# Norm 1's factors amid V, dt's softplus a unit sooner, decay sums inside z, x's convolution behind z's splits

## The chip, the cores and the metric

One Trainium2 chip, one NeuronCore of it. The metric is device time in microseconds of one launch, the median of several runs. Engines are named as in the profile: PE is TensorE (matrix products; PEld its weight loads), DVE is VectorE, ACT is ScalarE, POOL is GpSimd, and SP is SyncE, which here only issues DMAs.

## What is computed

One hybrid decoder layer on 256 tokens of width 1024, in float32. What matters here is its beginning: norm 1, one combined input projection, and the SSD mixer with its `dt`.

```python
hn = rmsnorm(x, norm1_w)
proj = hn @ w_in
z, xbc_raw, dt_raw, q, k, v, g_raw = jnp.split(proj, IN_OFFSETS, axis=-1)
xbc = jax.nn.silu(causal_dwconv(xbc_raw, conv_w, conv_b))
xs, Bm, Cm = jnp.split(xbc, [SSD_D_INNER, SSD_D_INNER + SSD_GN], axis=-1)
dt = jax.nn.softplus(dt_raw + dt_bias)
Adt = dt * -jnp.exp(a_log)
A_cs = jnp.cumsum(Adt, axis=-1)      # per chunk of 128 tokens
L = jnp.exp(segsum(Adt))
y_diag = jnp.einsum('bclgn,bcsgn->bcgls', Cc, Bc) * L  @ (X * dt)
...
```

There are 32 SSD heads in 8 groups and 16 attention heads. After the mixer and the attention come the merge gates, an output projection, a ConvFFN with its own norm, and a last norm; the change touches none of these.

## The kernel before

**Units of weights.** Every projection is cut into units of 1 MB of weights: 8 pieces along the depth of 1024, each of 128 rows by 256 columns. SP loads a unit into one of three buffers `raw` (`load_raw`, line 90). Products are float32 by parts: ScalarE rounds half a unit (4 pieces) to its high part `hi` (`split_high`, line 95), VectorE subtracts to get the low part `lo` (`split_half`, line 101), and TensorE then does three products for each piece and column half: high by high, high by low, low by high (`mm_unit`, lines 160 to 162). A unit is thus 48 products. There are four buffers each for `hi` and `lo`. `next_unit` loads ahead and splits one unit ahead, so that a unit's splits are traced while the unit before it is multiplied.

**The order of the units.** For each of 8 groups `g`: B and C (`u_bc`), x (`u_x`), q and k (`u_qk`), z (`u_z`), and in turn V or the merge gates (`u_gate`). V's first unit and the first half of unit 0 (B and C of group 0) are special: they are multiplied before the splits are there, in plain float32.

**The head.** The input comes in four loads. `prepare` (lines 299 to 302) squares two pieces of x on ScalarE, scales them by the norm's weights on VectorE into `xw`, and adds the two squares. TensorE does V's products with the unnormalised `xw` (`v_raw`, line 289, two products a piece), the sums of squares with a column of ones (`stats`, line 306), and between them idle products (`idle`, line 295), whose result nobody reads. Then come the root (line 321, ScalarE), and the factor `rstd1` (lines 322 to 326, VectorE), dt's raw products (line 329), the factor's broadcast to all partitions (`rms_bcast`, line 237), and two idle products. `normed` (line 336) multiplies by the factor on VectorE, and the plain products of unit 0 (line 347) follow it piece by piece; then ScalarE and VectorE split the normalised input (`high`, `low`, lines 339 and 342) and the weights, and TensorE ends unit 0 with split products. In this stretch TensorE, ScalarE and VectorE keep the program's order.

**After the head.** From line 638 on only TensorE keeps the program's order. The order of ScalarE's and VectorE's queues is chosen when the kernel is built, by a planner that goes by what is ready and by priority (program order, unless a block is marked `high_priority`); `issue_after(i)` puts a block's instructions on the engine of `i` behind `i` in that engine's queue. `hn_end` holds the last high and the last low split of the head. `conv_silu` (lines 379 to 389) starts on ScalarE (`cacc`), does three taps for each of two halves on VectorE, a tanh on ScalarE, and a product on VectorE. `dt_chain` (line 597) turns dt's raw rows with four narrow instructions of TensorE (line 600) and then makes the softplus and dt times A in some twenty small steps, a chain on VectorE with two steps of ScalarE. `dt_sums` (line 622) makes the running sums over a chunk on TensorE, `dt_turn` (line 630) transposes them, copies them and writes them to DRAM on POOL's queue, and `load_acs` reads them back as a broadcast to all partitions (`acsB`). From these `s_mx` (line 469) makes the decay factors: twelve pieces on ScalarE, one exponential, and a product with B·C on VectorE. The scan's products `s_y` of group `g` are done behind x's unit of group `g + 1`.

**Banks.** Three PSUM banks pass round among the units' outputs (`mm_tile`); a unit's output holds one until the last of its readers is through. Other banks carry the tags `ss` (2), `at` (2) and `acc` (1).

**What the change touches:** `split_half`, the loop around `v_raw`, the place of `rms_bcast` and of dt's turn, `conv_silu`, `u_x`, `u_qk`, `u_z`, `s_mx`, `dt_chain`, and in the group loop what is done for `g` 0 and 1.

Of the kernel before, what the change touches and what calls it, by code (L numbers as in the profile page):

```python
# [8 lines left out]
F32 = mybir.dt.float32  # L9
F32R = mybir.dt.float32r  # L10
I32 = mybir.dt.int32
AF = mybir.ActivationFunctionType
# [29 lines left out]
def block_kernel(tc, xtok_d, head_d, par_d, nf_d, con_d, rope_d, win_d, wgate_d, bg_d, watt_d, wssd_d, wout_d, wup_d, wdn_d, out_d):  # L42
# [3 lines left out]
    with st:  # L46
# [33 lines left out]
        def col(c):  # L80
            return par[:, c : c + 1]
# [11 lines left out]
        def split_high(raw, k0, n):  # L93
            hi = wpool.tile([P, 4, 256], F32R, tag="hi", bufs=4, name="hi")
            split_half.hi = nc.scalar.activation(hi[:, :n], raw[:, k0 : k0 + n], AF.Copy)  # L95
            return hi

        def split_half(raw, k0, n, hi=None):
            hi = hi or split_high(raw, k0, n)
            lo = wpool.tile([P, 4, 256], F32R, tag="lo", bufs=4, name="lo")  # L100
            split_half.lo = nc.vector.tensor_tensor(lo[:, :n], raw[:, k0 : k0 + n], hi[:, :n].bitcast(F32),  # L101
                                                    op=ALU.subtract)
            return hi, lo, n

        def split_unit(raw, nk=KD):

# [174 lines left out]
        with tc.manual_schedule(engines=IN_ORDER):  # L281
# [22 lines left out]
            def stats(k, first=False, last=False):  # L304
                for c in range(2):
                    nc.tensor.matmul(stat[:, 0, c : c + 1], sq[:, k, c * P : c * P + P], ones[:, 0:1],
                                     start=(first and c == 0), stop=(last and c == 1))

            for k in range(0, KD, 2):
                prepare(k)  # L310
            for k in range(0, KD, 2):
                v_raw(k)
                if k == 6:
                    stats(6, last=True)
                v_raw(k + 1)
                if k < 6:
                    stats(k, first=(k == 0))
                    idle((3, 2, 1)[k // 2])

            mh, root, rr = n1[:, 0], n1[:, 1], n1[:, 2]  # L320
            nc.scalar.activation(root, stat[:, 0, 0:2], AF.Sqrt, scale=1.0 / D, bias=eps)
# [2 lines left out]
            nc.vector.tensor_tensor(rr, root, root, op=ALU.mult)  # L324
            nc.vector.tensor_tensor(rr, rr, mh, op=ALU.mult)
            nc.vector.scalar_tensor_tensor(rstd1, rr, 1.5, root, op0=ALU.add, op1=ALU.mult)
            for k in range(KD):
                j = NH * (k % 4)
                nc.tensor.matmul(ps_dt[j : j + NH, 0, :], wdt[:, k], xw[:, k], start=(k < 4), stop=(k >= KD - 4))
            rb1 = rms_bcast(rstd1)  # L330
            idle(2)

            psbc = mm_tile()

# [18 lines left out]
            for k in range(4, KD):  # L353
                low(k)
            half0 = split_half(raws[0], 4, 4, hi)
            mm_unit(psbc, [half0], hn, first=False, k0=4)
            nc.scalar.activation(dtp, ps_dt[:, 0, :], AF.Copy)
            for c in range(2):
                nc.scalar.activation(vt0[:, c], psv[:, c], AF.Identity, scale=rstd1[:, c : c + 1])
            for k in range(4):  # L360
# [9 lines left out]
                nc.vector.tensor_scalar(par[:, a:b], par[:, a:b], 0.5, None, op0=ALU.mult)  # L370


        def conv_silu(dst, src, cts, urgent=False):
# [3 lines left out]
            with tc.high_priority() if urgent else ExitStack():  # L377
                for m in range(2):
                    i = nc.scalar.activation(accs[m], src[:, m], AF.Identity, bias=col(C_CB + cts[m]), scale=w(m, 3))  # L379
            conv_silu.first = i  # L380
            for m in range(2):
                acc = accs[m]
                for s in (1, 2, 3):
                    i = nc.vector.scalar_tensor_tensor(acc[:, s:], src[:, m, : T - s], w(m, 3 - s), acc[:, s:],  # L384
                                                       op0=ALU.mult, op1=ALU.add)
                conv_silu.taps = i
# [9 lines left out]
        def u_bc(g):  # L396
            hv = next_unit()
            ps = mm_tile() if g else psbc
            if g:
                mm_unit(ps, hv, hn)  # L400
            bc = S[g]["bc"] = ssp.tile([P, 2, T], F32, tag="bc", bufs=1, name="bc")
            conv_silu(bc, ps, (16 + g, 24 + g), urgent=(g == 1))

        def u_x(g):
            hv = next_unit()
            ps = mm_tile()
            mm_unit(ps, hv, hn)
            xs = S[g]["xs"] = ssp.tile([P, 2, T], F32, tag="xs", bufs=2, name="xs")
            conv_silu(xs, ps, (2 * g, 2 * g + 1))

        def load_acs(g):
            acsB = S[g]["acsB"] = ssp.tile([P, 4, T], F32, tag="acsB", bufs=1, name="acsB")
# [1 line left out]

        def u_qk(g):
            hv = next_unit()
            ps = mm_tile()
            mm_unit(ps, hv, hn)
            raw = atp.tile([P, 2, T], F32, tag="qkraw", bufs=1, name="qkraw")
            S[g]["qk_copy"] = nc.scalar.activation(raw, ps, AF.Copy)  # L420
            sw = swaps[g % 2]
            nc.gpsimd.dma_start(sw[48:80:2], raw[49:80:2])
            nc.gpsimd.dma_start(sw[49:80:2], raw[48:80:2])
            qk = S[g]["qk"] = atp.tile([P, 2, T], F32, tag="qk", bufs=2, name="qk")
            cosb = rope[:, 0:1, :].to_broadcast([P, 2, T])
            nc.vector.tensor_tensor(qk, raw, cosb, op=ALU.mult)
# [22 lines left out]
            vt = S[g - 1]["vt"] = S[g]["vt"] = ssp.tile([P, 2, T], F32, tag="vt", bufs=2, name="vt")  # L449
            nc.scalar.activation(vt, ps, AF.Copy)  # L450

        def u_z(g):
            hv = next_unit()
            ps = mm_tile()
            mm_unit(ps, hv, hn)
            zt = S[g]["zt"] = ssp.tile([P, 2, T], F32, tag="zt", bufs=2, name="zt")
            S[g]["z_tanh"] = nc.scalar.activation(zt, ps, AF.Tanh, scale=0.5)
            nc.vector.scalar_tensor_tensor(flat(zt), flat(zt), 1.0, flat(ps), op0=ALU.add, op1=ALU.mult)
# [7 lines left out]
            nc.vector.tensor_tensor(cb, pcb[:, 0:3], mmask, op=ALU.mult)  # L466
            S[g]["cb"] = cb

        def s_mx(g, behind, conv=()):
# [5 lines left out]
            def factors(r):  # L475
                h = 4 * g + r
                for c, b in ((0, 0), (1, 2)):
                    nc.scalar.activation(mx[:, r, b], acsB[:, r, c * P : c * P + P], AF.Relu, scale=-1.0,
                                         bias=acs[:, c, h : h + 1])
                nc.scalar.activation(mx[:, r, 1], acsB[:, r, P:T], AF.Exp, bias=alm[:, h : h + 1])  # L480

            with ExitStack() as order:
                order.enter_context(tc.issue_after(behind.ins))
                factors(0)
                factors(1)
                if conv:
                    order.enter_context(tc.high_priority())
                    order.enter_context(tc.issue_after(conv[0].ins))
                    order.enter_context(tc.issue_after(conv[1].ins))
                factors(2)  # L490
                factors(3)
                nc.scalar.activation(mx[:, :, 0:3:2], mx[:, :, 0:3:2], AF.Exp, scale=-1.0)
                m2 = mx.rearrange("p h b l -> p h (b l)")
                nc.vector.tensor_tensor(m2, m2, flat(cb)[:, None, :].to_broadcast([P, 4, 3 * P]), op=ALU.mult)

        def s_xt(g):
            xs = S[g]["xs"]
# [97 lines left out]
        b3 = lambda ap: ap[:, None, :].to_broadcast([P, 2, NH])  # L595
        r3 = lambda i: dtw[:, i].rearrange("p (c h) -> p c h", c=2)
        def dt_chain():
            ps = ps_s.tile([P, 2, T], F32, tag="ss", bufs=2, name="ps_dt2")
            for c in range(2):
                nc.tensor.matmul(ps[:, 0, c * NH : c * NH + NH], dtp[:, c * P : c * P + P], sel, start=True, stop=True)  # L600
            for c in range(2):
                nc.vector.scalar_tensor_tensor(dtw[:, 0, c * NH : c * NH + NH], ps[:, 0, c * NH : c * NH + NH],
                                               rstd1[:, c : c + 1], par[:, C_DTB : C_DTB + NH], op0=ALU.mult, op1=ALU.add)
            nc.scalar.activation(dtw[:, 1], dtw[:, 0], AF.Abs)
            nc.scalar.activation(dtw[:, 2], dtw[:, 1], AF.Exp, scale=-1.0)
# [87 lines left out]
        for g in range(NG):  # L693
            if g:
                u_bc(g)
                with ExitStack() as order:
# [364 lines left out]
```

## Time and profile before

| | us |
|---|---|
| median of 3 runs (600.14 to 601.01) | 600.63 |
| the profiled execution, its time | 600.57 |
| the profiled execution, its span in the trace | 598.8 |
| TensorE busy in the span | 586.7 |
| VectorE busy | 459.7 |
| ScalarE busy | 375.9 |

The trace covers the span; the 1.8 us that the time has over it lie around the span. Times in rows are microseconds from the span's start. In timelines an entry in brackets is the idle time of the engine in front of the instruction, and what ended it. A row can merge several alike instructions (x8); its length is then that of the whole run of them. Matmuls overlap: one is shown with 0.28 us, yet the next starts 0.12 later.

### The profile page before, as it was taken

Reading aid. Unit: us, or ns where it says so; the run is one execution under the profiler, and the core shown is the slowest. Engines: PE = TensorE matmul, PEld = TensorE weight load, DVE = VectorE, ACT = ScalarE, POOL = GpSimd, SP = SyncE. Lnnn points to the kernel's source line nnn. Section 1 sums busy time; section 2 is a strip of 40 time slices with the busy share of each in tenths; the row PEclk is TensorE's granted clock in tenths of the full one; section 3 lists DMA queues with packets and bytes.
Section 4 is the critical chain, followed back from the end, with each engine's and each line's share of the span. In section 5 each row is a group of like instructions: output and inputs, shape, how many; then the busy total and the mean of one; then the engine's idle time right before and its main releaser. Section 6 shows DMA issues by size and latency. Waiting matters only on the chain.

```text
span 598.8 us, 9952 instructions
## 1 busy us (share of the span) xinstructions
PE 586.7 (98%) x3840; PEld 526.2 (88%) x3840; DVE 459.7 (77%) x891; ACT 375.9 (63%) x673; POOL 21.2 (4%) x41
## 2 busy tenths in 40 slices
PE   9999999999999999999999999999999999999994
PEld 8798989999999999999998888889888888888884
DVE  2798689879797897978987546767888988884643
ACT  2754785966769567695687334456877777774432
POOL 0020000100001000010000000000000000000100
PEclk9999999999999999999999999999999999999999
DMA  8549456474473644636435756545455555464611
GB/s 308 210 132 337 136 190 195 112 296 141 146 245 108 251 142 150 242 113 245 141 107 180 268 196 204 181 170 184 169 210 187 175 201 202 130 216 163 225 51 71
DMA packets 17936, 109.74 MB, mean 183 GB/s; under 512 B 2256, under 2 KB 2512, under 8 KB 6240
## 3 DMA queue, kind: packets, MB, share of 16 engines
q1 hardware_dynamic: 15120, 100.42, 47.8%
q0 software_dynamic: 2336, 6.85, 4.3%
q10 hardware_dynamic: 432, 1.84, 0.8%
q8 instruction: 30, 0.49, 0.3%
q14 instruction: 18, 0.15, 0.1%
HBM read 107.49 MB, written 1.08 MB: 181 GB/s over the span
## 4 chain that ended last, share of the span: by engine, by line
PE 94%; DVE 4%; ACT 1%; DMA 1%; issue 0%; ACTq 0%; DVEq 0%
PE up L170 12%; PE mm L191 11%; PE mm L193 11%; PE mm L192 11%; PE mm L162 10%; PE mm L160 10%; PE mm L161 10%; PE up L174 6%; PE py L516 2%; PE mm L289 1%; PE po L582 1%; PE s_ps L545 1%; DVE cacc L384 1%; PE pb L237 1%; DVE lo L101 1%; PE mm L445 1%
## 5 line engine op out<-in xcount | busy, mean ns | idle before, releaser
L95 ACT ACTIVATE hi<-raw 128x1024 fp32r<-128x1024 f32 x183 | 192.0, 1057 | 134.8 <-PE mm L193 63.0
L101 DVE TENSOR_TENSOR lo<-raw,hi 128x1024 fp32r<-128x1024 f32 x183 | 222.9, 1224 | 68.5 <-ACT hi L95 66.7
L162 PE MATMUL mm<-hn,lo 128*128 128x256 f32 x504 | 143.0, 284 | 3.2 <-DVE lo L101 3.2
L160 PE MATMUL mm<-hn,hi 128*128 128x256 f32 x504 | 143.6, 285 | 0.0
L161 PE MATMUL mm<-hn,hi 128*128 128x256 f32 x504 | 142.6, 283 | 0.0
L162 PEld LDWEIGHTS mm<-hn,lo 128*128 128x128 f32 x504 | 96.6, 192 | 4.1 <-DVE lo L101 4.1
L160 PEld LDWEIGHTS mm<-hn,hi 128*128 128x128 f32 x504 | 96.6, 192 | 0.9 <-ACT hi L95 0.4
L161 PEld LDWEIGHTS mm<-hn,hi 128*128 128x128 f32 x504 | 96.7, 192 | 0.2
L170 PE MATMUL up<-xw,hi 128*128 128x512 f32 x320 | 76.3, 391 | 0.0
L170 PEld LDWEIGHTS up<-xw,hi 128*128 128x128 f32 x320 | 58.8, 188 | 11.4
L384 DVE SCALAR_TENSOR_TENSOR cacc<-mm,par,cacc 128x255 f32<-128x255 f32 (+2 forms) x96 | 44.6, 476 | 5.3 <-ACT cacc L379 4.4
L174 PEld LDWEIGHTS up<-xw,lo 128*128 128x128 f32 x320 | 41.0, 191 | 1.6
L174 PE MATMUL up<-xw,lo 128*128 128x256 f32 x320 | 41.5, 283 | 0.0
L192 PE MATMUL mm<-lo,act 128*128 128x512 f32 (+1 forms) x92 | 35.0, 380 | 0.0
L191 PE MATMUL mm<-hi,act 128*128 128x512 f32 (+1 forms) x92 | 34.9, 380 | 0.0
L193 PE MATMUL mm<-hi,act 128*128 128x512 f32 (+1 forms) x92 | 34.9, 380 | 0.0
L878 DVE SCALAR_TENSOR_TENSOR facc<-ab,par,facc 128x255 f32<-128x255 f32 (+1 forms) x44 | 21.3, 483 | 11.3 <-ACT facc L876 10.6
L191 PE MATMUL mm<-hi,hn 128*128 128x512 f32 x64 | 25.5, 398 | 0.0
L191 PE MATMUL mm<-hi,yn 128*128 128x512 f32 x64 | 25.2, 394 | 0.0
L193 PE MATMUL mm<-hi,hn 128*128 128x512 f32 x64 | 25.0, 391 | 0.0
L192 PE MATMUL mm<-lo,hn 128*128 128x512 f32 x64 | 25.0, 390 | 0.0
L193 PE MATMUL mm<-hi,yn 128*128 128x512 f32 x64 | 24.9, 390 | 0.0
(208 smaller groups left out, 972.6 us busy)
## 6 DMA issues: line engine op xcount, KB each, us to landing
raw<-in_win_dram SPq DMA_DIRECT2D x34, 1024.0 KB, 4.9
raw<-in_wup_dram SPq DMA_DIRECT2D x22, 1024.0 KB, 4.8
raw<-in_wdn_dram SPq DMA_DIRECT2D x10, 1024.0 KB, 4.9
raw<-in_wgate_dram SPq DMA_DIRECT2D x8, 1024.0 KB, 5.4
raw<-in_wssd_dram SPq DMA_DIRECT2D x8, 1024.0 KB, 5.0
acsB<-acsT_d POOLq DMA_DIRECT2D x8, 512.0 KB, 5.5
raw<-in_watt_dram SPq DMA_DIRECT2D x4, 1024.0 KB, 5.4
raw<-in_wout_dram SPq DMA_DIRECT2D x4, 1024.0 KB, 5.3
```

Source lines behind the costliest of these rows:

```text
L95: split_half.hi = nc.scalar.activation(hi[:, :n], raw[:, k0 : k0 + n], AF.Copy)
L101: split_half.lo = nc.vector.tensor_tensor(lo[:, :n], raw[:, k0 : k0 + n], hi[:, :n].bitcast(F32), op=ALU.subtract)
L160: nc.tensor.matmul(ps[m], wh, xh, start=a, stop=False)
L161: nc.tensor.matmul(ps[m], wh, xl, start=False, stop=False)
L162: nc.tensor.matmul(ps[m], wl, xh, start=False, stop=z)
L170: nc.tensor.matmul(ps[:, m].rearrange("p a b -> p (a b)"), hi[:, kk, m * P : m * P + P], act[k].rearrange("p a b -> p (a b)"), start=(k == ...
L174: nc.tensor.matmul(ps[:, m, 1], lo[:, kk, m * P : m * P + P], act[k][:, 0, :], start=False, stop=(k == len(tiles) - 1))
L191: nc.tensor.matmul(o, xh, wh, start=(k == 0 if apart else k0 + k == 0), stop=False)
L192: nc.tensor.matmul(o, xh, wl, start=False, stop=False)
L193: nc.tensor.matmul(o, xl, wh, start=False, stop=(k0 + k == nk - 1))
L384: i = nc.vector.scalar_tensor_tensor(acc[:, s:], src[:, m, : T - s], w(m, 3 - s), acc[:, s:], op0=ALU.mult, op1=ALU.add)
L878: nc.vector.scalar_tensor_tensor(acc[:, s:], src[:, : T - s], w(2 - s), acc[:, s:], op0=ALU.mult, op1=ALU.add)
```

## The change

In the head, V's parts are multiplied singly and the sums of squares come earlier among them; the factor's broadcast stands ahead of V's last part and of dt's raw products; of eight idle products four are left.

```diff
-            for k in range(0, KD, 2):
+            for k in range(4):
                 v_raw(k)
-                if k == 6:
-                    stats(6, last=True)
-                v_raw(k + 1)
-                if k < 6:
-                    stats(k, first=(k == 0))
-                    idle((3, 2, 1)[k // 2])
+                if k % 2:
+                    stats(k - 1, first=(k == 1))
+                    idle(3 if k == 1 else 1)
+            stats(4)
+            v_raw(4)
+            stats(6, last=True)
+            v_raw(5)
+            v_raw(6)
...
+            rb1 = rms_bcast(rstd1)
+            v_raw(7)
             for k in range(KD):
                 j = NH * (k % 4)
                 nc.tensor.matmul(ps_dt[j : j + NH, 0, :], wdt[:, k], xw[:, k], start=(k < 4), stop=(k >= KD - 4))
-            rb1 = rms_bcast(rstd1)
-            idle(2)
```

dt's raw rows are copied and turned ahead of unit 0's split products, on a bank of tag `at`, and `dt_chain` starts from there, right behind the head's last splits, ahead of x's unit in the program.

```diff
             half0 = split_half(raws[0], 4, 4, hi)
+            nc.scalar.activation(dtp, ps_dt[:, 0, :], AF.Copy)
+            ps_dt2 = ps_s.tile([P, 2, T], F32, tag="at", bufs=2, name="ps_dt2")
+            for c in range(2):
+                nc.tensor.matmul(ps_dt2[:, 0, c * NH : c * NH + NH], dtp[:, c * P : c * P + P], sel, start=True, stop=True)
             mm_unit(psbc, [half0], hn, first=False, k0=4)
-            nc.scalar.activation(dtp, ps_dt[:, 0, :], AF.Copy)
...
+        with tc.high_priority(), tc.issue_after(hn_end[0]), tc.issue_after(hn_end[1]):
+            dt_chain()
         u_x(0)
-        with tc.high_priority():
-            dt_chain()
```

x's convolution of group 0 is put behind the second low half of z's weights on VectorE. z's unit is issued in two halves, with the decay sums between them in group 0, and the sums' transposes follow z at once.

```diff
         def u_x(g):
...
-            conv_silu(xs, ps, (2 * g, 2 * g + 1))
+            if g:
+                conv_silu(xs, ps, (2 * g, 2 * g + 1))
+            else:
+                S[g]["x_ps"] = ps
...
         def u_qk(g):
             hv = next_unit()
+            if g == 0:
+
+                with tc.issue_after(split_half.lo.ins):
+                    conv_silu(S[0]["xs"], S[0]["x_ps"], (0, 1))
...
-        def u_z(g):
+        def u_z(g, between=None):
             hv = next_unit()
             ps = mm_tile()
-            mm_unit(ps, hv, hn)
+            mm_unit(ps, hv[:1], hn, last=False)
+            if between:
+                between()
+            mm_unit(ps, hv[1:], hn, first=False, k0=4)
...
             if g == 0:
-                u_z(g)
+                u_z(g, dt_sums)
+                dt_turn()
                 turn_qk(g)
-                dt_sums()
                 gate = u_gate(0)
                 next(gate)
-                dt_turn()
                 load_acs(0)
```

In group 1 the decay factors of group 0 are ordered behind the last but one high split (`last_hi`) alone, and no longer split by the start of B/C's convolution; that convolution has no priority of its own any more (`urgent` is gone), and x's unit is no longer ordered behind its first step.

```diff
         def split_half(raw, k0, n, hi=None):
             hi = hi or split_high(raw, k0, n)
+            split_half.last_hi = split_half.hi_before
+            split_half.hi_before = split_half.hi
...
                 u_bc(g)
-                with ExitStack() as order:
-                    if g == 1:
-                        s_mx(0, split_half.hi, (conv_silu.first, conv_silu.taps))
-                        order.enter_context(tc.issue_after(conv_silu.first.ins))
-                    u_x(g)
+                if g == 1:
+                    s_mx(0, split_half.last_hi)
+                u_x(g)
```

## Rows read from the trace of the kernel before

**Rows 1.** The page, the engines' busy time, share of the span and instructions

```profile
PE 586.7 (98%) x3840; PEld 526.2 (88%) x3840; DVE 459.7 (77%) x891; ACT 375.9 (63%) x673; POOL 21.2 (4%) x41
```

**Rows 2.** TensorE's waits over the span: us in total, times, longest

```profile
PE mm L162 <- DVE lo L101: 3.2, 3, 1.4
```

**Rows 3.** The chain of waits, 0 to 60 us: start, us, engine, output, line

```profile
10.68 0.55 PE idle L295 x4
...
13.30 0.33 PE idle L295 x2
13.63 0.87 PE mm L289 x4
14.50 0.34 PE stat L306 x4
...
15.81 1.00 PE ps_dt L329 x16
16.81 0.66 PE pb L237 x4
...
31.92 0.36 PE ps_dt L600 x4
...
40.00 0.39 DVE cacc L384
```

**Rows 4.** Timeline of the head, 0 to 32 us: start, us, engine, line, operation

```profile
1.06 4.21 PE L78 MATMUL warm<-ones 128*128 128x128 f32 x18 [1.06 <-DVE eps L282]
...
14.87 0.26 ACT L321 ACTIVATE n<-stat,eps 128x2 f32<-128x2 f32 x1 [4.44 <-PE stat L306]
...
15.83 0.16 DVE L326 SCALAR_TENSOR_TENSOR n<-n 128x2 f32<-128x2 f32 x1
...
17.49 2.74 DVE L336 TENSOR_TENSOR sq<-xw,pb 128x256 f32<-128x256 f32 x8 [1.50 <-PE pb L237]
...
17.96 3.72 PE L347 MATMUL mm<-sq,raw 128*128 128x256 f32 x16
...
21.69 1.23 DVE L101 TENSOR_TENSOR lo<-raw,hi 128x1024 fp32r<-128x1024 f32 x1
...
24.86 2.36 DVE L101 TENSOR_TENSOR lo<-raw,hi 128x1024 fp32r<-128x1024 f32 x2 [0.43 <-ACT hi L95]
```

**Rows 5.** Timelines of VectorE and TensorE at z's unit of group 0

```profile
40.96 1.22 DVE L101 TENSOR_TENSOR lo<-raw,hi 128x1024 fp32r<-128x1024 f32 x1
...
42.66 0.22 DVE L620 TENSOR_TENSOR dtw<-dt,nega 128x64 f32<-128x64 f32 x1
...
40.96 0.28 PE L161 MATMUL mm<-hn,hi 128*128 128x256 f32 x1
42.23 0.38 PE L162 MATMUL mm<-hn,lo 128*128 128x256 f32 x1 [1.00 <-DVE lo L101]
```

**Rows 6.** Timeline of TensorE at the start of z's unit of group 1

```profile
77.53 0.28 PE L160 MATMUL mm<-hn,hi 128*128 128x256 f32 x1
77.65 0.28 PE L161 MATMUL mm<-hn,hi 128*128 128x256 f32 x1
79.37 0.39 PE L162 MATMUL mm<-hn,lo 128*128 128x256 f32 x1 [1.44 <-DVE lo L101]
```

**Rows 7.** Timeline of ScalarE, 18 to 66 us

```profile
31.90 1.06 ACT L95 ACTIVATE hi<-raw 128x1024 fp32r<-128x1024 f32 x1 [0.83 <-PE mm L161]
...
51.21 0.35 ACT L635 ACTIVATE acsT<-ps_t 32x256 f32<-32x256 f32 x1
...
61.06 0.69 ACT L478 ACTIVATE mx<-acsB,acs 128x128 f32<-128x128 f32 x2 [1.01 <-DMA acsB<-acsT_d]
```

**Rows 8.** The chain of waits, 64 to 82 us

```profile
64.71 0.49 DVE cacc L384
...
67.65 1.36 DVE mx L494
```

**Rows 9.** Busy time of each engine in a stretch of the head, with TensorE's granted clock (PEclk), DMA share

```profile
12.00:14.00 2.00, 2.00 (x14) 1.84 (x13) 0.00 (x0) 0.00 (x0) 0.00 (x0) 1.00 1.08 428
```

More of the change, by code (lines that the diff above doesn't have):

```diff
@@ L103, in split_half @@
             return hi, lo, n
+        split_half.hi_before = None
         def split_unit(raw, nk=KD):
@@ L370, in block_kernel, with conv_silu @@
                 nc.vector.tensor_scalar(par[:, a:b], par[:, a:b], 0.5, None, op0=ALU.mult)
-        def conv_silu(dst, src, cts, urgent=False):
+        def conv_silu(dst, src, cts):
             accs = [work.tile([P, T], F32, tag="cacc", bufs=4, name="cacc") for _ in range(2)]
             w = lambda m, j: col(C_CW + 4 * cts[m] + j)
[L377 to L380, printed above, removed]
+            for m in range(2):
+                nc.scalar.activation(accs[m], src[:, m], AF.Identity, bias=col(C_CB + cts[m]), scale=w(m, 3))
             for m in range(2):
@@ L383, in conv_silu @@
                 for s in (1, 2, 3):
-                    i = nc.vector.scalar_tensor_tensor(acc[:, s:], src[:, m, : T - s], w(m, 3 - s), acc[:, s:],
-                                                       op0=ALU.mult, op1=ALU.add)
-                conv_silu.taps = i
+                    nc.vector.scalar_tensor_tensor(acc[:, s:], src[:, m, : T - s], w(m, 3 - s), acc[:, s:],
+                                                   op0=ALU.mult, op1=ALU.add)
                 th = work.tile([P, T], F32, tag="tanh", bufs=2, name="th")
@@ L401, in u_bc @@
             bc = S[g]["bc"] = ssp.tile([P, 2, T], F32, tag="bc", bufs=1, name="bc")
-            conv_silu(bc, ps, (16 + g, 24 + g), urgent=(g == 1))
+            conv_silu(bc, ps, (16 + g, 24 + g))
         def u_x(g):
@@ L467, in s_cb, with s_mx @@
             S[g]["cb"] = cb
-        def s_mx(g, behind, conv=()):
+        def s_mx(g, behind):
             acsB, cb = S[g]["acsB"], S[g]["cb"]
             mx = S[g]["mx"] = ssp.tile([P, 4, 3, P], F32, tag="mx", bufs=1, name="mx")
[L475 to L480, printed above, removed]
-            with ExitStack() as order:
[L483 to L491, printed above, removed]
+            with tc.issue_after(behind.ins):
+                for r in range(4):
+                    h = 4 * g + r
+                    for c, b in ((0, 0), (1, 2)):
+                        nc.scalar.activation(mx[:, r, b], acsB[:, r, c * P : c * P + P], AF.Relu, scale=-1.0,
+                                             bias=acs[:, c, h : h + 1])
+                    nc.scalar.activation(mx[:, r, 1], acsB[:, r, P:T], AF.Exp, bias=alm[:, h : h + 1])
                 nc.scalar.activation(mx[:, :, 0:3:2], mx[:, :, 0:3:2], AF.Exp, scale=-1.0)
-                m2 = mx.rearrange("p h b l -> p h (b l)")
-                nc.vector.tensor_tensor(m2, m2, flat(cb)[:, None, :].to_broadcast([P, 4, 3 * P]), op=ALU.mult)
+            m2 = mx.rearrange("p h b l -> p h (b l)")
+            nc.vector.tensor_tensor(m2, m2, flat(cb)[:, None, :].to_broadcast([P, 4, 3 * P]), op=ALU.mult)
         def s_xt(g):
@@ L597, in dt_chain @@
         def dt_chain():
-            ps = ps_s.tile([P, 2, T], F32, tag="ss", bufs=2, name="ps_dt2")
             for c in range(2):
-                nc.tensor.matmul(ps[:, 0, c * NH : c * NH + NH], dtp[:, c * P : c * P + P], sel, start=True, stop=True)
-            for c in range(2):
-                nc.vector.scalar_tensor_tensor(dtw[:, 0, c * NH : c * NH + NH], ps[:, 0, c * NH : c * NH + NH],
+                nc.vector.scalar_tensor_tensor(dtw[:, 0, c * NH : c * NH + NH], ps_dt2[:, 0, c * NH : c * NH + NH],
                                                rstd1[:, c : c + 1], par[:, C_DTB : C_DTB + NH], op0=ALU.mult, op1=ALU.add)
@@ L695, in block_kernel @@
                 u_bc(g)
-                with ExitStack() as order:
-                    if g == 1:
-                        s_mx(0, split_half.hi, (conv_silu.first, conv_silu.taps))
-                        order.enter_context(tc.issue_after(conv_silu.first.ins))
-                    u_x(g)
+                if g == 1:
+                    s_mx(0, split_half.last_hi)
+                u_x(g)
                 small_1(g)
```

## The prediction

> **What bounds the kernel now.** I read the engines' shares first: TensorE is busy for 586.7 of 598.8 us, VectorE for 459.7 [rows 1]. So the time is TensorE's own work plus what it waits for. TensorE's list of waits is short: low halves of weights, three times, 3.2 us in all [rows 2]. The chain of waits shows the head as one line on TensorE: V's parts, sums of squares, idle products, dt's products, the broadcast [rows 3]. What hangs on that line is seen in the timeline of the head: the root starts at 14.87, after ScalarE had stood 4.44 with the squares done at 10.43; normalising starts at 17.49; the first split half of unit 0 is complete at 22.92 (21.69 + 1.23) [rows 4]. Two larger waits come later: z's unit of group 0 at 42.23 (1.00 by the row) and z's of group 1 at 79.37 (1.44) [rows 5, 6]. After those no wait is listed, so what is won before 80 us is kept to the end; the weights' loads start when low halves free their buffers, and those move forward too.
>
> The sum is made against the profiled execution, 600.57 us with its span of 598.8; the median of the runs is 600.63, 0.06 above. A difference under 0.2%, 1.2 us, counts as none: about what a measurement of this kernel can tell.
>
> **Norm 1.** I walk the new order on TensorE from 10.68, where the second pair's idle products begin [rows 3]. One idle product in place of two: 0.33, to 11.01 (the row of two instructions, which are one product). Sums of the third pair, 0.34, to 11.35; V's fifth part, 0.87, to 12.22; last sums, 0.34, to 12.56; two more parts of V, 1.74, to 14.30 [rows 3]. The squares are there for both sums: done at 10.43, with one addition behind them. So the root starts at 12.6. From root to factor it is 15.99 - 14.87 = 1.12 [rows 4]; the factor is there at 13.7, 0.6 before TensorE comes to its broadcast. That takes 0.66 [rows 3], and normalising starts at 14.98 instead of 17.49: VectorE and ScalarE gain 2.51. TensorE meanwhile does V's last part and dt's products, 0.87 + 1.00, and reaches unit 0's plain products at 16.83 instead of 17.96. These are 16, spaced (3.72 - 0.39) / 15 = 0.22 (one alone shows 0.39) [rows 4, 6], so 3.56, to 20.39. Now the moved turn of dt, 0.36 [rows 3], to 20.75; the copy that it needs stands on ScalarE right behind the high half that the low half waits for, and is covered by that low half. The low half is complete at 22.92 - 2.51 = 20.41, so TensorE doesn't wait for it any more. The 24 split products left of unit 0 and the 48 of x's unit lie 0.12 apart (77.53 to 77.65 [rows 6]), 8.64: x's unit ends at 29.39. Now it ends at 31.92, and dt's turn behind it at 32.28 [rows 3]. **First term: 2.89.** The least is the 1.1 that TensorE's own order gives at 16.83, if the splits did not follow; the most 3.2, if a product less waits somewhere. I take 2.89: every step of it is a row, moved.
>
> **z's unit of group 0.** Its second low half starts on VectorE at 40.96, though ScalarE had the high half at 32.96 (31.90 + 1.06) [rows 5, 7]. Between them stand dt's chain and both convolutions. x's six taps now go behind that half. Without them (0.39 each [rows 3]) and one product of like shape, the half starts at 40.96 - 2.51 - 7 x 0.39 = 35.7 and ends at 36.9. TensorE starts qk at 29.39, z at 35.2 (48 products, 5.8), comes to z's second half at 38.0, and wants this low half after the decay sums (four narrow products, priced as dt's turn: 0.36) and two more, at 38.6. So the wait goes: 42.23 - 40.96 - 0.12 = 1.15, and 0.10 of restart (the matmul after it took 0.38, its neighbour 0.28) [rows 5]. **Second term: 1.25.**
>
> The sums are a new wait of TensorE: the queue is in order, so if they are late all of z, the gates and what follows stand behind them. They need dt's last product, which ended at 42.88 [rows 5], 10.6 after dt's turn at 32.28. Its chain may now begin behind the last low half of x's weights, 27.22 - 2.51 = 24.7 [rows 4]; with the same 10.6 it ends at 35.3, 2.7 before it is wanted. Bounds 0 to 2; I take 0.
>
> x's convolution also holds one of three banks, which the gates want at 38.4 + 2.9 + 0.2 = 41.5. Its taps from 36.9: 2.34, and should one low half (1.23 [rows 4]), qk's product (half that size, 0.6) and two small reads of the sums (0.16 each, as the factor's steps [rows 4]) come between, they end at 41.4. That is level. Bounds 0 to 1.2; I take 0, since the low half is later in the program than the taps.
>
> **Group 1.** dt's sums, turned, are copied at 51.21, by a ScalarE that had waited with a high half in front [rows 7]. The rows come back as a broadcast by 61.06, 9.5 after the copy's end (51.56). Now the transposes follow z directly, at 41.3; the copy ends at 42.0, the rows land at 51.5. Twelve factors at 0.35 (0.69 for two) and one exponential like a high half, 1.06, make 5.2, to 56.7; the product of 1.36 on VectorE [rows 8], to 58.1. What is queued behind the waiting factors on ScalarE is the second high half for x's unit and the gates' two tanh: the half is wanted when x's unit is half through, by about 62, so some 3 us are free. The product thus leaves the stretch from B/C's first tap (64.71, then 64.71 - 2.89 - 1.25 = 60.6) to 79.37, in which the chain lies on VectorE. Of its 14.7 us 1.36 go; and one low half, 1.2, is no longer ordered behind the convolution's first step and can run ahead. TensorE's wait there is 79.37 - 77.65 - 0.12 = 1.60, with 0.10 of restart [rows 6]; 2.5 us less work there covers it. **Third term: 1.70.** Bounds 0 to 1.9 (the scan's products wait a little too); I take 1.70, the row's own, as both edits relieve the engine that the chain names.
>
> **Little else.** The same TensorE work is done, less four idle products, which are in the walk. No DMA is added. The one that writes dt's sums keeps its place on POOL's queue behind the swaps and gate biases. The turned dt's bank is of another tag, free by then. In the other groups z's two halves keep their order. **Sum:** 2.89 + 1.25 + 1.70 = 5.84, and 0.2 back for small restarts at the new order's seams: 600.57 - 5.64 = 594.9.
>
> **Rivals.**
> *Queues late in group 0.* A planner chooses VectorE's and ScalarE's order, and no row shows the new one. If dt's steps or x's taps slip behind one or two low halves, TensorE stands at the decay sums or at the gates' bank for 1.2 to 3 us: 596.1 to 597.9, say 597.1. For it: the level sum above. Against: dt's steps have priority.
> *Group 1's wait stays,* since B/C's convolution there loses its priority and VectorE's stretch only moves: 594.9 + 1.7 = 596.6. Against: 2.5 us of that stretch leave.
> *The change doesn't do what it says:* z's half stays behind x's taps, the factors behind their load, and a stand at the sums eats norm 1's gain: about 600.
> *The clock falls.* Of eight idle products in the head four stay. TensorE's first 18 matmuls lay 0.23 apart (4.21 [rows 4]), idle ones of the same shape later 0.11 ((0.55 - 0.33) / 2 [rows 3]): the two paces. From 11.0 to 20.75 there are 9.7 us of work; all at the slow pace costs 9.7 and gives 604.6, and past 6.8 us of it (5.6 + 1.2) the kernel is slower than before. Against: V's parts fill the place, so TensorE is as busy as now (2.00 of 2.00 us, granted clock 1.00, the 2.4 GHz level [rows 9]). The Trainium skill (TensorE: Matmul & The Clock Gate, Part 1) says that the array is throttled by default and that activity releases it; by that rule taking out idle products is this change's dangerous edit, unless real work stands in for them.
>
> **Numbers.** Forecast (594 to 596) 0.52; late queues 0.22; group 1 0.14; no change 0.06; clock 0.06. Faster by over 0.2%: 0.52 + 0.22 + 0.14 = 0.88; within 0.06; slower 0.06. The range goes down to the high bounds (3.2 + 1.25 + 1.9 = 6.35, and 0.4 for steps I can't see: 593.8) and up to the end of the late queues, 598.0; the last two rivals are left out, 0.12.
>
> **What would show it.** Right: normalising starts at about 15.0; no wait before unit 0's split products; x's unit ends at 29.4; no wait listed in z of group 0; the factors begin near 51.5; none in z of group 1. Wrong: TensorE waiting before the decay sums for VectorE's dt product or before the gates for a tap; a low half again behind taps; normalising after 16; a granted clock under 1.00 before 25 us.

## The result and the profile after

The changed kernel takes 595.34 us (median of 4 runs, 595.12 to 595.69) beside 600.73 for the kernel before on the same chip: a ratio of 0.9912, with a 95% interval of 0.9895 to 0.9929. The forecast was 594.9, in a range of 593.8 to 598.0. The profiled execution has a span of 593.5 against 598.8, 5.3 less.

The page of the changed kernel, the engines' line (it answers to [rows 1]):

```profile
PE 584.9 (99%) x3832; PEld 525.8 (89%) x3832; DVE 458.8 (77%) x891; ACT 375.6 (63%) x673; POOL 21.2 (4%) x41
```

TensorE's list of waits over the whole span (it answers to [rows 2]), which has only the first warm-up product:

```profile
PE warm L78 <- DVE eps L286: 1.1, 1, 1.1
```

All three waits for low halves are gone, and none has come in their place. Eight instructions are missing, the four idle products. The chain of waits of the changed kernel, 0 to 60 us (it answers to [rows 3]):

```profile
5.27 2.81 PE mm L293 x8
...
8.42 0.78 PE idle L299 x6
...
11.26 0.33 PE idle L299 x2
...
12.90 0.34 PE stat L310 x4
13.24 1.83 PE mm L293 x8
15.08 0.44 PE pb L241 x4
15.52 0.87 PE mm L293 x4
16.39 1.00 PE ps_dt L337 x16
17.39 3.65 PE mm L353 x16
21.04 0.36 PE ps_dt L365 x4
...
38.76 0.17 PE ps_a L624 x2
38.92 0.20 PE ps_a L625 x2
42.07 0.22 PE ps_t L633 x2
```

One line of TensorE, as walked, without a hole: the last sums end at 13.24, the broadcast stands at 15.08, V's last part and dt's products behind it. But every entry comes 0.6 to 0.8 us later than walked, from the first products on. The same chain of the kernel before begins so, and has two more landmarks (rows not shown so far):

```profile
5.39 2.11 PE mm L289 x8
...
45.13 0.17 PE ps_a L624 x2
...
85.14 0.43 PE pcb L463 x2
...
98.80 1.45 PE py L516 x16
```

V's first four products took 2.81 in the one execution and 2.11 in the other. They are the same eight instructions on the same data; the changed part begins behind them. The two landmarks in the changed kernel's chain, 60 to 110 us:

```profile
79.85 0.43 PE pcb L479 x2
...
93.51 1.45 PE py L519 x16
```

From the end of V's first four products (7.50 and 8.08) to the scan's products in the round of group 2 it is 91.30 before and 85.43 after: 5.87 less. The sum of the prediction's three terms was 5.84. The difference to 5.3 in the span is those first products, which end 0.58 later (8.08 against 7.50).

Where the work of the other engines went, in the changed kernel's timelines of VectorE and ScalarE (they answer to [rows 4, 5, 7]):

```profile
15.56 2.74 DVE L342 TENSOR_TENSOR sq<-xw,pb 128x256 f32<-128x256 f32 x8 [1.17 <-PE pb L241]
...
19.76 1.23 DVE L103 TENSOR_TENSOR lo<-raw,hi 128x1024 fp32r<-128x1024 f32 x1
...
25.21 0.40 DVE L602 SCALAR_TENSOR_TENSOR dtw<-ps_dt,n,par 128x32 f32<-128x32 f32 x2
...
34.80 1.22 DVE L103 TENSOR_TENSOR lo<-raw,hi 128x1024 fp32r<-128x1024 f32 x1
...
36.98 0.21 DVE L620 TENSOR_TENSOR dtw<-dt,nega 128x64 f32<-128x64 f32 x1
...
41.25 0.47 DVE L391 SCALAR_TENSOR_TENSOR cacc<-mm,par,cacc 128x253 f32<-128x253 f32 x1
...
61.16 1.76 DVE L497 TENSOR_TENSOR mx<-mx,cb 128x1536 f32<-128x1536 f32 x1 [1.35 <-ACT mx L495]
62.83 2.35 DVE L103 TENSOR_TENSOR lo<-raw,hi 128x1024 fp32r<-128x1024 f32 x2
65.10 1.90 DVE L391 SCALAR_TENSOR_TENSOR cacc<-mm,par,cacc 128x255 f32<-128x255 f32 x4
66.92 1.22 DVE L103 TENSOR_TENSOR lo<-raw,hi 128x1024 fp32r<-128x1024 f32 x1
...
69.30 1.22 DVE L103 TENSOR_TENSOR lo<-raw,hi 128x1024 fp32r<-128x1024 f32 x1
...
42.96 0.35 ACT L635 ACTIVATE acsT<-ps_t 32x256 f32<-32x256 f32 x1
...
54.56 0.70 ACT L492 ACTIVATE mx<-acsB,acs 128x128 f32<-128x128 f32 x2 [2.91 <-DMA acsB<-acsT_d]
```

Normalising starts at 15.56 (17.49 before), z's second low half of group 0 ends at 36.0 (42.2), dt's last product at 37.2 (42.9). The factors begin at 54.56, not at 51.5 as predicted, and their product at 61.16. The two low halves for q and k of group 1 run at 62.83, ahead of the first tap of B/C's convolution (65.10). z's low halves of group 1, the last two `lo` rows shown, run at 66.92 and 69.30. In VectorE's timeline of the kernel before, with its first tap at 64.71, the same ones (the two for q and k, then z's first) are:

```profile
69.91 2.36 DVE L101 TENSOR_TENSOR lo<-raw,hi 128x1024 fp32r<-128x1024 f32 x2
...
78.09 1.22 DVE L101 TENSOR_TENSOR lo<-raw,hi 128x1024 fp32r<-128x1024 f32 x1
```

### The profile page after: what moved, and what is told of

Same layout as the page of the kernel before. It is cut to its first block, busy times and chain, and to the rows that moved or that the text cites. A ratio compares the mean times of both kernels' runs of the same rounds, so it can differ in the third digit from the quotient of the medians.

```text
span 593.5 us, 9945 instructions
## 1 busy us (share of the span) xinstructions
PE 584.9 (99%) x3832; PEld 525.8 (89%) x3832; DVE 458.8 (77%) x891; ACT 375.6 (63%) x673; POOL 21.2 (4%) x41
## 4 chain that ended last, share of the span: by engine, by line
PE 99%; DVE 0%; issue 0%; ACT 0%; DVEq 0%; ACTq 0%
PE up L174 12%; PE mm L164 11%; PE mm L165 11%; PE mm L166 11%; PE mm L195 11%; PE mm L196 11%; PE mm L197 11%; PE up L178 6%; PE py L519 2%; PE mm L293 1%; PE s_ps L548 1%; PE po L585 1%; PE mm L458 1%; PE mm L459 1%; PE mm L460 1%; PE pt_ps L571 1%
## 5 line engine op out<-in xcount | busy, mean ns | idle before, releaser
L875 DVE SCALAR_TENSOR_TENSOR facc<-ab,par,facc 128x255 f32<-128x255 f32 (+1 forms) x44 | 21.2, 483 | 11.4 <-ACT facc L873 10.6
L195 PE MATMUL mm<-hi,yn 128*128 128x512 f32 x64 | 25.2, 394 | 0.0
```

The source lines that it names most:

```text
L195: nc.tensor.matmul(o, xh, wh, start=(k == 0 if apart else k0 + k == 0), stop=False)
L875: nc.vector.scalar_tensor_tensor(acc[:, s:], src[:, : T - s], w(2 - s), acc[:, s:], op0=ALU.mult, op1=ALU.add)
```

## The experiments

Each one edits the changed kernel. Since V's first four products differ from execution to execution, I compare besides the medians the distance from their end to the scan's products of the round of group 2 in the profiled executions ("the distance", 85.43 in the changed kernel). From that landmark to the end of the span it is 500.0 us in every profile here, the kernel before's too. A median also holds those first products, which alone differ by up to 1 us between executions, so of a difference under 1 us the distance says more than the median.

**The head's old order (e1_norm_back).**

```diff
...
-            for k in range(4):
...
-            v_raw(6)
+            for k in range(0, KD, 2):
+                v_raw(k)
+                if k == 6:
+                    stats(6, last=True)
+                v_raw(k + 1)
+                if k < 6:
+                    stats(k, first=(k == 0))
+                    idle((3, 2, 1)[k // 2])
...
-            rb1 = rms_bcast(rstd1)
...
+            rb1 = rms_bcast(rstd1)
+            idle(2)
```

> The changed kernel with the head's old order alone: V's parts in pairs, sums behind them, eight idle products, the factor's broadcast behind dt's raw products. My theory (the order of the head is worth what the walk gave): normalising starts at about 17.5 instead of 15.6, TensorE waits again for the low half of unit 0, dt's turn of 0.36 still lies in that wait, so x's unit ends about 2.5 us later than by the walk and the time is 2 to 2.6 us over the changed kernel's 595.3, 597.3 to 597.9; z's wait in group 0 and group 1's stay away. Rival (only TensorE's own order counts, the splits are ready either way): 1.1 us, 596.4.

597.91 us (ratio to before 0.9963, interval 0.9951 to 0.9975), 2.6 over the changed kernel: the theory's upper figure, though the ten runs reach from 597.13 to 600.85. Normalising starts at 17.26. The distance is 88.64, 3.2 longer; 2.4 of it stand already at the decay sums (40.33 - 7.28 against 38.76 - 8.08), the theory's 2.5. The other 0.8 comes behind the sums; in group 1 TensorE's weight loads wait 0.5 for attention's probabilities and some 0.2 twice; the rest is not accounted for. Ahead of unit 0's split products TensorE waits 0.3, and for dt's copied rows, not for the low half. So the order of the head is worth 2.4 with dt's turn still covered (the first term, 2.89, counts that turn's 0.36 too), and TensorE's own 1.1 is not the whole of it.

**x's convolution back in x's unit (e2_conv_back).**

```diff
         def u_x(g):
-            if g:
-                conv_silu(xs, ps, (2 * g, 2 * g + 1))
-            else:
-                S[g]["x_ps"] = ps
+            conv_silu(xs, ps, (2 * g, 2 * g + 1))
```

> The changed kernel with x's convolution of group 0 back in x's unit, free to go ahead of z's low half. My theory (that half was late because x's taps stood ahead of it): the wait in z of group 0 is back with 1 to 1.3 us, 596.3 to 596.6. Rival (with dt's chain begun a unit sooner VectorE has room enough, and the place of the convolution is worth nothing): no wait, 595.3.

597.08 us (0.9944, 0.9929 to 0.9959): the wait is back. Timeline of TensorE in this run:

```profile
37.04 0.39 PE L166 MATMUL mm<-hn,lo 128*128 128x256 f32 x1 [1.73 <-DVE lo L103]
...
38.33 0.28 PE L164 MATMUL mm<-hn,hi 128*128 128x256 f32 x1
...
39.01 0.41 PE L165 MATMUL mm<-hn,hi 128*128 128x256 f32 x1
39.22 0.41 PE L166 MATMUL mm<-hn,lo 128*128 128x256 f32 x1
```

and the stretch behind the wait, busy times and (third number from the end) TensorE's granted clock, with the stretch after it:

```profile
38.00:42.00 4.00, 4.00 (x24) 4.00 (x23) 2.93 (x6) 1.06 (x1) 0.60 (x2) 0.57 0.65 124
42.00:46.00 4.00, 4.00 (x31) 3.76 (x31) 3.66 (x6) 1.31 (x3) 0.00 (x0) 1.00 0.98 386
```

The wait is 1.73, at z's first low half already, and it has a second price. From 38.6 to 42.0 the granted clock stands at its lower level (1.2 GHz) and the products lie 0.21 apart instead of 0.12. The distance is 3.51 longer: 1.7 of waiting and 1.7 of slow products. The four runs lie between 596.5 and 597.99, the profiled one on top. Its mean granted clock is 0.993, that of the other three 0.996 to 0.998, so they seem to have paid the wait alone: 1.2 to 1.9 us over the changed kernel.

**Group 1 as before (e3_factors_back).** The old `s_mx` with its split factors, the priority of B/C's convolution, and x's unit behind that convolution's first step:

```diff
-                if g == 1:
-                    s_mx(0, split_half.last_hi)
-                u_x(g)
+                with ExitStack() as order:
+                    if g == 1:
+                        s_mx(0, split_half.hi, (conv_silu.first, conv_silu.taps))
+                        order.enter_context(tc.issue_after(conv_silu.first.ins))
+                    u_x(g)
```

> The changed kernel with group 0's decay factors, the priority of B/C's convolution of group 1 and the order of x's unit as before. My theory (this is the third term): the wait at z of group 1 is back with some 1.7 us, 597.0. Rival (the wait went because everything before came sooner, and the factors' place is not what counts): no wait, 595.3.

596.67 us (0.9934, 0.9917 to 0.995), 1.3 over the changed kernel. TensorE's waits, 0 to 110 us, have the old one again:

```profile
PE mm L166 <- DVE lo L103: 1.4, 1, 1.4
```

The distance is 1.73 longer, which is the third term (1.70). Which of the three edits carries it, the next ones ask.

**Only x's unit tied again, with the convolution's priority (e6_x_tied).**

```diff
-            conv_silu(bc, ps, (16 + g, 24 + g))
+            conv_silu(bc, ps, (16 + g, 24 + g), urgent=(g == 1))
...
-                u_x(g)
+                with ExitStack() as order:
+                    if g == 1:
+                        order.enter_context(tc.issue_after(conv_silu.first.ins))
+                    u_x(g)
```

> The changed kernel, but B/C's convolution of group 1 has its priority back and x's unit of group 1 (its splits among it) is again ordered behind that convolution's first step; the factors stay where the change put them. If the third term comes from the low halves that may now run ahead of the convolution: the wait at z of group 1 is back with about 1.7 us, 596.7 to 597. If it comes from the factors' place (the prediction's first reason): no wait, 595.3.

597.95 us (0.995, 0.9929 to 0.9971), but with runs from 595.03 to 600.82. The profiled one, 599.87, shows how a long one comes about. Its timelines of ScalarE and TensorE, and the stretch behind with the granted clock:

```profile
58.05 0.69 ACT L495 ACTIVATE mx<-acsB,acs 128x128 f32<-128x128 f32 x2 [6.82 <-DMA acsB<-acsT_d]
```

```profile
80.04 0.38 PE L166 MATMUL mm<-hn,lo 128*128 128x256 f32 x1 [2.15 <-DVE lo L103]
```

```profile
81.00:85.00 4.00, 4.00 (x22) 3.88 (x21) 2.06 (x3) 3.97 (x11) 0.36 (x1) 0.57 0.95 326
```

Here the sums' rows landed at 58.0 instead of 54.5. ScalarE stood 6.8 us for them. Behind the factors stood the second high half for x's unit, and behind the convolution's first step the splits that are traced inside x's unit, those for q and k. z's low half was 2.15 late, and the clock fell again behind that wait, 81.2 to 84.6. The distance is 90.46, 5.0 longer. The ten runs go with their mean granted clock: the five from 598.61 up have 0.993 to 0.995, the four up to 596.19 have 0.996 to 0.998. So with the tie and the priority the wait is back; how large it is differs from execution to execution.

**The complement, factors split, x's unit free (e7_factors_split).**

```diff
-                    s_mx(0, split_half.last_hi)
+                    s_mx(0, split_half.hi, (conv_silu.first, conv_silu.taps))
                 u_x(g)
```

> The complement: the factors split by the convolution as before, and the convolution with its priority, but x's unit of group 1 free. If the third term comes from the factors' place: the wait is back, 596.7 to 597. If from the low halves: no wait, 595.3.

596.05 us (0.9923, 0.9908 to 0.9938). Neither: no wait for a low half, but a new one (TensorE's waits, 0 to 110 us), at the scan's products, for the factors' product:

```profile
PE py L535 <- DVE mx L513: 1.1, 1, 1.1
```

With x's unit free, z's low halves are in time; with the factors split, their product is late. The distance is 1.18 longer. The third term needs both. (The convolution's priority came back together with the split; which of the two makes the product late, no run tells.)

**The tie alone, without priority (e10_tie_alone).**

```diff
-                u_x(g)
+                with ExitStack() as order:
+                    if g == 1:
+                        order.enter_context(tc.issue_after(conv_silu.first.ins))
+                    u_x(g)
```

> The changed kernel with x's unit of group 1 ordered behind the first step of B/C's convolution, and nothing else (no priority for that convolution). The run with priority and tie waited 2.1 us for a low half and spread from 595.0 to 600.8, and there the rows of the sums landed only at 58.0. If the tie itself holds back the low halves: a wait at z of group 1 of 1 to 2 us, 596.3 to 597.5. If it was the late landing of that one execution: no wait when the rows land near 54.5, 595.3.

595.74 us (0.9924, 0.9902 to 0.9946), runs from 594.5 to 599.07. In the profiled one the rows landed near 54.9, and TensorE waited 0.3 for a low half (0.5 on its weight loads); the distance is 0.61 longer. With the rows at that time the tie costs 0.6 us. A late landing without the tie costs little too: in the run with the factors behind the last high half, below, the rows landed at 57.4 and the wait was 0.4. So the 2.15 of e6 took more than either; that it was both together, and not the priority, is argued, not shown. The longest run here, 599.07, has a granted clock of 0.993 against 0.996 and 0.997, which points to a fall of the clock in it as in e6, but there is no profile of it. The wide spread is not the tied kernels' alone: the head's old order (600.85, clock 0.994) and the run with one warm-up product less (598.87, 0.994) have long runs as well.

**dt's chain back behind x's unit (e5_dt_back).**

```diff
-        with tc.high_priority(), tc.issue_after(hn_end[0]), tc.issue_after(hn_end[1]):
-            dt_chain()
         u_x(0)
+        with tc.high_priority():
+            dt_chain()
```

(dt's turn goes back into `dt_chain` too.)

> The changed kernel with dt's turn and its chain back behind x's unit, in the program as before; the sums stay between z's halves. My theory (the sums can stand inside z only because dt begins a unit sooner): the chain starts near 30.5, takes 8 to 10.6 us and is late for sums wanted at 38.8; TensorE stands at the sums for 0.5 to 2.2 us, 595.8 to 597.5. Rival (VectorE has little else to do since x's taps are behind z's low half, so that the chain is fast): no wait at the sums, 595.3.

596.8 us (0.9935, 0.9918 to 0.9951). TensorE's waits over this run's span:

```profile
PE ps_a L624 <- DVE dtw L620: 1.4, 1, 1.4
```

The new wait that the prediction priced at 0 to 2 is there as soon as dt is late; the distance is 1.96 longer (the turn, 0.36, is no longer covered either). Its chain ran from 29.9 to 39.9, 10.0, close to the 10.6 that the prediction carried over.

**The sums back behind z (e8_sums_back).**

```diff
-                u_z(g, dt_sums)
-                dt_turn()
+                u_z(g)
                 turn_qk(g)
+                dt_sums()
                 gate = u_gate(0)
                 next(gate)
+                dt_turn()
```

> The changed kernel with the sums behind z and their transposes inside the gates, as before. If the sums' place matters by itself: the rows of the sums come back some 5 us later than at 54.6, ScalarE stands for them with the high halves for x's unit of group 1 behind it, and TensorE waits 0.5 to 2 us in group 1, 595.8 to 597.3. If there is room for that: no wait, 595.3.

595.11 us (0.9908, 0.9893 to 0.9923), no wait, the distance 85.46. Nothing is lost, and the timeline of ScalarE says why:

```profile
54.48 0.70 ACT L492 ACTIVATE mx<-acsB,acs 128x128 f32<-128x128 f32 x2 [2.67 <-DMA acsB<-acsT_d]
```

The rows land at the same time although they are sent 3 us later. POOL's timelines of the changed kernel and, in the second fence, of this one:

```profile
43.60 0.52 POOL L636 DMA_DIRECT2D acsT_d<-acsT  x1 [3.31 <-ACT acsT L635]
48.42 0.55 POOL L422 DMA_DIRECT2D acsB<-acsT_d  x1 [4.30 <-DMA acsT_d<-acsT]
```

```profile
46.61 0.52 POOL L636 DMA_DIRECT2D acsT_d<-acsT  x1 [6.19 <-ACT acsT L635]
48.63 0.56 POOL L422 DMA_DIRECT2D acsB<-acsT_d  x1 [1.51 <-DMA acsT_d<-acsT]
```

The read follows the landing of the 32 KB written: it is issued at 48.42 and at 48.63, though the write was issued at 43.60 and at 46.61. By the DMA packets of the two traces a load of 1 MB of weights is in flight from 43.9 to 47.7 in the changed kernel and from 43.1 to 47.8 here; the write's packets move from 47.1 to 47.8 and from 47.7 to 48.0. So in both kernels the small write is through when that load is. The read's packets, too, move only from 51.8 and 52.0 on, when most of the next load (48.7 to 52.5 and 48.8 to 52.4) is through.

**The factors behind the last high half (e11_last_high).**

```diff
-                    s_mx(0, split_half.last_hi)
+                    s_mx(0, split_half.hi)
```

> The changed kernel with group 0's decay factors behind the last high half (x's second, group 1) instead of the one before it. My theory: that half no longer stands behind factors that wait for their load (54.6 in the changed kernel's trace), but TensorE wants it only at some 62, so it is worth nothing: 595.3, no new wait; the factors' product on VectorE comes up to 1 us sooner. Rival (the planner's order turns on it): the factors fall behind B/C's convolution and the scan's products wait 1 us or more, 596.3 or above.

595.06 us (0.9906, 0.9894 to 0.9919): worth nothing, as expected. In its profiled execution, the longest of the four runs, the rows landed only at 57.4, TensorE waited 0.4 for a low half, and the distance is 0.68 longer.

**No idle products (e4_no_idle).**

```diff
                     stats(k - 1, first=(k == 1))
-                    idle(3 if k == 1 else 1)
```

> The changed kernel without the four idle products left in the head. If real work keeps TensorE at its full pace: the head is shorter by their 0.78 + 0.33, the input pieces are there (VectorE has scaled the second by 7.7, the third by 9.1), the root starts 1.1 us sooner and the time is 594.2. If the idle products are needed for the pace, products behind them lie 0.43 apart instead of 0.22 for some us and the time is 596 to 599; the first rival of the prediction on the clock would then be alive.

593.62 us (0.9888, 0.9873 to 0.9903), the fastest kernel of this study: its runs lie from 593.59 to 594.4, all under the changed kernel's lowest, 595.12. The chain of waits of this run:

```profile
5.28 2.83 PE mm L293 x8
8.11 0.34 PE stat L310 x4
8.45 1.83 PE mm L293 x8
10.28 0.79 PE stat L310 x8
...
14.21 0.44 PE pb L241 x4
```

V's parts keep 0.22 between two instructions behind the missing idle products, and the broadcast stands 0.87 earlier. The distance is 0.90 shorter, and that is what the idle products cost; the median is 1.72 lower. The profiled run, with 2.83 for V's first products, is the longest of the four; the other three are 0.8 shorter, about what those products can differ by, but no profile of them shows it. TensorE is at its full pace without the idle products.

**No idle products and one warm-up product less (e9_no_idle_warm8).**

```diff
-WARM = 9
+WARM = 8
```

> The changed kernel without idle products in the head and with one warm-up product less (8 instead of 9). Theory: the run without idle products showed TensorE with no wait from the head on, so only work taken out of it counts; the last warm-up product ends at 5.27 where the first scaled input is there at 5.1, so up to 0.2 us more: 593.3 to 593.6. Rival (the warm-up sets when the array comes to its full pace, so a product less brings that later and V's first products are slower): 593.8 to 594.5.

595.02 us (0.991, 0.9889 to 0.9931), runs from 593.57 to 598.87. V's first products start at 5.21, not at 5.28, and take 2.98; the distance is 84.66 against 84.53. Nothing is won; whether the warm-up product or chance made these runs wide is open.

**No idle products, the sums behind z (e12_no_idle_sums_back).** The edits of e4 and e8 together.

> The changed kernel without idle products in the head and with the sums behind z, their transposes inside the gates. From the two single runs: idle products cost their 0.9 us of TensorE's time and the sums' place costs nothing, so 593.4 to 594.4, no wait of TensorE before 80 us, and the sums' rows land within 1 us of where they land with the sums inside z. Rival (the sums' early place has been room that the shorter head now needs): a wait at the scan's products or at z of group 1, 595 or above.

594.77 us (0.9905, 0.9889 to 0.9922), 1.1 over e4, so the rival is nearer. The distance is 85.36, 0.8 longer than e4's 84.53, with waits of 0.7 on TensorE's weight loads for attention's probabilities in group 1. The sums' place, free in the changed kernel, seems not to be free once the head is shorter. How it makes these waits is open: the rows land at 53.8, in the run without idle products alone at 53.7, and up to the scan's products of the round of group 1 the two traces are level to 0.1.

## Why the prediction was right, and where it was not

**Norm 1.** The walk holds line by line: from the end of V's first products, the root starts 5.2 later (13.28), the walk had 5.1 (12.6 - 7.5); normalising 7.48 later, the walk 7.48; unit 0's low half is complete at 20.99, before TensorE's 21.4. x's unit ends at 21.40 + 8.64 = 30.04, 2.24 before where dt's turn ended before (32.28); with the 0.58 of V's first products it is 2.82 of the 2.89.

What was not in the sum is those first products. They took between 1.99 and 2.98 in the thirteen profiled executions of changed kernels, 2.11 in the kernel before. In the trace the granted clock's first record (full speed) begins at 5.67 us in the kernel before and at 7.08 in the changed kernel; over all fourteen profiles it begins at 3.92 to 7.24. In the five in which it begins before the products do (3.92 to 5.04) they take 1.99. In the nine others, from 5.67 on, they take 2.11 to 2.98, the longer, to within 0.05, the later it begins: in front of it they lie 0.43 apart, behind it 0.22. (A window of the profile reads 1.00 for the clock in front of the first record too; there only the distance of the products tells the level.) This is chance of the execution, not the edit: the instructions before it are the same, but for one warm-up product in e9. The prediction walked from 10.68 in one execution, and so took the end of these products there as fixed.

**z of group 0.** By the sums' end and the transposes (45.13 + 0.37 + 0.22 = 45.72 before, 42.29 after) the lead grows from 2.24 to 3.43: 1.19 against the predicted 1.25. The low half ended at 36.0 (predicted 36.9) and was wanted at about 39. dt was done at 37.2, 1.4 before the sums began (38.59), where the prediction had 2.7: the chain did not start at 24.7 but at 25.2, behind the splits, and took 12. The margin was real and half as large; e5 shows the wait that appears without it. x's taps ended at 41.7 and the gates wanted the bank at 42.3, level but in time, as reckoned.

**Group 1.** The lead grows from 3.43 to 5.29 (85.14 against 79.85), 1.86 with the small wait at the scan's products; predicted was 1.70, and the bound 1.9. The size is right, but the first half of the reason, the times at which the factors come, is wrong. The step that failed is "the rows land at 51.5"; they landed at 54.5. Of these 3.0 us 1.3 lie in front: ScalarE copied the turned sums by 43.3 and not by 42.0, again with a high half in front. The way through DRAM was carried over as 9.5 from the row before, and took 11.2: the write took about as long as before (the read that waits for it was issued 4.8 us behind it, 5.1 before), the read back 6.1 instead of 4.1. Its packets began to move 3.4 us after its issue, with most of a load of weights through (e8); in the kernel before they began 1.3 us after it (58.2). So the factors' product came at 61.16, not at 56.7. It is still ahead of the first tap, but that came at 65.10 and not at 60.6, behind the product and the two low halves for q and k. What saves the wait is the second half of the reason, and more of it than the one low half reckoned: both low halves for q and k run ahead of the taps, and z's, at 66.92 and 69.30, among them. e7 shows that freeing these alone moves the wait to the scan's products, so both edits are needed: the tie alone costs 0.61 (e10), the split factors with the priority 1.18 (e7), together 1.79, beside 1.73 for both (e3).

**The sum.** The terms came out at 2.82, 1.19 and 1.86 where the prediction had 2.89, 1.25 and 1.70. That their sum, 5.87, meets 5.84 so closely is in part luck, as the errors cancel. The 0.2 that the forecast gave back for restarts does not show in the distance, and the 0.58 of chance in the first products left the span 5.3 shorter.

**The rivals.** Late queues in group 0 and a change that doesn't do what it says: not seen. Group 1's wait for a low half: only with the old order (e3, 1.4), the tie (e6, 2.15; e10, 0.3) or a late landing of the sums' rows (e11, 0.4). The clock rival was wrong about its cause: e4 has no idle product in the head at all and no fall; V's parts are work enough. That agrees with the Trainium skill (TensorE: Matmul & The Clock Gate, Part 1), by which the array is throttled by default and activity releases it. What did bring a fall here is a wait: after 1.73 (e2) and 2.15 (e6) the granted clock stood at the lower level for 3.4 us, after 1.4 (e3, e5) and the 1.44 of the kernel before it did not.

## What to carry over

Where one engine in program order bounds the kernel, a walk along it with rows of the trace can give the change closely (here to 0.2 us for each term), provided each moved wait is checked against who supplies it. Let the sums that a late factor needs go first among independent products of the same engine, and put the independent rest behind the broadcast. And take a landing time from a row only with the traffic that row had: a small write issued 3 us earlier into busy DMA engines landed no earlier. Filler work may have become a cost: the four idle products left were worth nothing and took 0.9 us.

## What the runs showed of the hardware

- A wait of TensorE can cost twice: behind waits of 1.73 and 2.15 us the granted clock stood at 1.2 GHz for 3.4 us, which cost 1.7 us more (e2: the distance grew by 3.51). Behind waits of 1.4 none was seen.
- The instant when the granted clock first comes to full speed varied from 3.92 to 7.24 us after the span's start among fourteen executions with equal warm-up products (one had one less), and V's first four products took between 1.99 and 2.98 us by it. That is the size of many a gain looked for here.
- The broadcast of the sums (512 KB from DRAM) landed 4.1 us after its issue before the change, and 5.0 (e2) to 9.0 us (e6) after it in the changed kernels. In the changed kernel and in e8 its packets began to move 3.4 us after the issue, when most of a load of weights in flight was through; in the kernel before they began 1.3 us after it.
